# Gate rows by a strided DMA, and nineteen steps of dot products in the second down product

## The chip, the cores and the metric

The kernel runs on one core of a Trainium2 chip. The metric is the device time of one execution in microseconds (us); the median of a few runs is compared. A profile of one execution gives the engines' busy times, their waits and the clock granted to TensorE. The engines are called TensorE (PE in the profile; PEld is its weight load), VectorE (DVE), ScalarE (ACT), GpSimd (POOL) and SyncE (SP, which here only issues DMAs).

## What is computed

One layer of a diffusion backbone: 512 latent tokens and 256 context tokens of width 1024, with shift, scale and gate vectors made from a conditioning vector (`c` for the latent tokens, `c_ctx` for the context). Cut to what matters here:

```python
mod_x = (jax.nn.silu(c) @ w_ada + b_ada).reshape(bsz, N_MOD, 1, d)      # N_MOD = 9 sections of 1024
mod_c = (jax.nn.silu(c_ctx) @ w_ada + b_ada).reshape(N_MOD, 1, d)

def ffn_sublayer(h, m, i, w_up, w_down):
    shift, scale, gate = sub_mod(m, i)                                  # sections 3i, 3i+1, 3i+2
    y = swiglu(modulate(h, shift, scale), w_up, w_down)                 # 1024 -> 2 x 2816 -> 1024
    return post_ln(DEEPNORM_ALPHA * h + 0.5 * gate * y, ln_g[i], ln_b[i])

x = ffn_sublayer(x, mod_x, 0, ffn1_w_in, ffn1_w_out)
ctx = ffn_sublayer(ctx, mod_c, 0, ffn1_w_in, ffn1_w_out)
...                       # neighbourhood attention and gated DeltaNet on sections 3 and 4
x = post_ln(DEEPNORM_ALPHA * x + gate_x * branch_merge(...), ln_g[1], ln_b[1])     # section 5
x = ffn_sublayer(x, mod_x, 2, ffn2_w_in, ffn2_w_out)                    # sections 6, 7, 8
```

The context's output isn't wanted, so the context needs sections 0 to 4 only.

## The kernel before

Matmuls take split operands: a float32 value is written as a high and a low part (`split`, lines 137 and 139: ScalarE casts, VectorE subtracts), and each product is three matmuls. The first half-step's hidden width of 2816 is 22 tiles of 128. The first 8 tiles (`N1`) are computed unit by unit, for the latent tokens and then for the context (`ffn_unit`, lines 192 to 194). Their part of the down projection follows (`down`, line 211): the *first down product*, first for the latent tokens ("x": eight weights, two of them held and used tile by tile at the end), then for the context ("c"). The result goes to DRAM as `accd`. The other 14 tiles (`N2`) are computed by `Seven.run`, a product of seven block products in place of eight (lines 527 to 529); each unit's hidden tile goes to DRAM as `hd`. Then the *second down product* (lines 672 to 674) reads these back as `hx` and `hc`, splits them, and adds the other 14 weights' share: 24 matmuls of 512 columns for a weight, the last six weights (`KL1`) held and used tile by tile. The context's share follows, then the input projection and the mixers.

The conditioning's sections 0 and 1 are made at the start (`modulate_k`). Sections 2 to 8 come from a generator, `ada_gen` (line 291). Each of its 56 steps loads 128 columns of `w_ada` (transposed, 512 KB) into a raw tile, and VectorE multiplies it with a broadcast conditioning row and sums (`dot_cols`, line 281): one dot product for sections 5 to 8, two (latent, context) for sections 2 to 4. The sums stand as columns, 128 partitions by 8, in `colx` and `colc`; at a section's end the bias is added (line 303). `ada_step(n)` runs n steps where it stands in the program. The steps are laid out so: two in the latent units, six in the context units, six in the first down product (`t_sums`, called after each of its first six weights), and 42 in the sevenfold units (`ADA2`).

Gates (sections 2, 5 and 8, and section 2 for the context) are needed as rows along the free dimension. `rows_out` does this for all sections that are ready, at two places: after the context units, and after the sevenfold units. `to_row` transposes 8 columns on TensorE (line 242), scales by 0.5 on ScalarE (line 244) and writes 8 rows of 512 bytes to DRAM (line 245); later a broadcast DMA loads the row for all partitions (lines 564, 248).

Each engine runs its instructions in order, and so does each DMA queue issue its transfers. That order is laid down when the kernel is built: the program's instructions are scheduled against a simulated timeline, so an instruction can be placed ahead of one that stands earlier in the program, if its operands and buffers are ready first by that simulation. SP's queue carries the weights (line 174), the generator's raw tiles (line 297), the hidden tiles (line 656) and the gate rows; POOL's queue carries `hd` and `accd`. Weights come through a `Stream` with two raw tiles and, here, three pairs of split tiles.

The generator's raw tiles during the sevenfold units:

```python
    def raw2():
        raws2[0] += 1
        return tl(tp, [P, D], "wr") if raws2[0] % 2 else tl(sgp, [P, D], "wr")
```

Memory comes in pools that open and close like a stack from either side; a tile in a newly opened pool waits for the last use of what lay there.

Of the kernel before, what the change touches and what calls it, by code (L numbers as in the profile page):

```python
# [12 lines left out]
AF = mybir.ActivationFunctionType  # L13
# [5 lines left out]
P = 128  # L19
D = 1024  # L20
KT = D // P
# [37 lines left out]
def body(ctx, tc, I, out, dbg=None):  # L59
    nc = tc.nc  # L60
    V, S, G, T = nc.vector, nc.scalar, nc.gpsimd, nc.tensor
# [15 lines left out]
    def tl(p, shape, tag, bufs=1, dt=F32):  # L77
        uid[0] += 1
        return p.tile(list(shape), dt, name=f"{tag}_{uid[0]}", tag=tag, bufs=bufs)
# [156 lines left out]
                        after(t, j, banks[t])  # L236
        return banks, tail

    def to_row(sp, pp, cols, row):

        ps = tl(pp, [8, P], "ps", 8)
        T.transpose(ps[:], cols, ident)
        t = tl(sp, [P, D], "adap")[0:8, 0:P]
        S.activation(t, ps[:], AF.Copy, scale=0.5)
        nc.sync.dma_start(row, t)

    def bcast_row(dst, row):
        nc.sync.dma_start(dst[:], row.rearrange("k p -> (k p)")[None].broadcast_to([P, D]))
# [42 lines left out]
    def ada_gen(tps, raw_of, crow):  # L291
        for sec in range(2, 9):
            which = [(0, colx)] + ([(1, colc)] if sec < 5 else [])
            sl = slice(sec * 8, sec * 8 + 8)
            for k in range(KT):
                raw = raw_of[0]()
                nc.sync.dma_start(raw[:], I["w_adaT"][sec * KT + k])
                for w, col in which:
                    dot_cols(tps[0], raw, crow[:, w], col, sec * 8 + k)
                if k < KT - 1:  # L300
                    yield
            for w, col in which:
                V.scalar_tensor_tensor(col[:, sl], col[:, sl], float(sec % 3 == 1), bcol[:, sl], op0=ALU.add, op1=ALU.add)
                if (w, sec) in gates:
                    rows_due.append((w, sec))
            yield

    def secs(col, s):
        return col[:, s * 8:s * 8 + 8]
# [72 lines left out]


    F0, KC, KL1, KL2 = 3, 2, 6, 6
    ADA2 = (2, 2, 2, 2, 3, 3, 3, 4, 4, 4, 4, 4, 5, 0)
    PSB = [2]
    pp0, close_pp0 = pool("pp0", space=PSUM)
    nc.scalar.dma_start(crow[0:1], I["c_row"])
# [51 lines left out]
        xn["c"].append(tl(st0, [P, D], f"x{t}")[:])  # L440
        ln_norm(tp, xn["c"][t], raw, act=True)
    gates = {k: tl(dp, [8, P], "gate")[:] for k in ((0, 2), (1, 2), (0, 5), (0, 8))}
    ada_tp, ada_raw, rows_due = [tp], [raw1], []
    ada = ada_gen(ada_tp, ada_raw, crow)

    def ada_step(n=1):
        for _ in range(n):
            next(ada, None)

    def rows_out(pp):  # L450
        while rows_due:
            w, sec = rows_due.pop(0)
            to_row(ada_tp[0], pp, secs((colx, colc)[w], sec), gates[(w, sec)])

    for f in range(F0, N1):
        hx.append(h_x())
        ffn_unit(tp, pp, ws.get(), ws.get(), uxh, uxl, NX, *hx[-1])
        for k in range(KC * (f - F0), min(KC * (f - F0 + 1), KT)):
            modulate_k(pp, "c", k)
        if f < F0 + 2:  # L460
            ada_step()
    trow = {}

    def sums(k):
# [11 lines left out]
    for f in range(N1):  # L476
        hc.append(h_c())
        ffn_unit(tp, pp, ws.get(), ws.get(), uch, ucl, NCT, *hc[-1])
        ada_step(f < 6)
    rows_out(pp)  # L480
    accd = tl(dp, [6, P, D], "accd")

    def t_sums(j):
        if j < 4:
            sums(j)
        ada_step()

    class Seven:

# [67 lines left out]
                r.prep_b()  # L557

    sraw = [tl(tp, [P, 3, 512], "s")[:].rearrange("p a n -> p (a n)")]
    for kind, n, hs in (("x", 4, hx), ("c", 2, hc)):  # L560
        g = [tl(tp, [P, 512], "fs", 2) for _ in range(2)]
        row = gates[(kind == "c", 2)].rearrange("k p -> (k p)")[None]
        for d in range(2):
            nc.sync.dma_start(g[d][:], row[:, d * 512:(d + 1) * 512].broadcast_to([P, 512]))
        banks, tail = down(pp, ws, hs, n, 2 if kind == "x" else 0, tail if kind == "c" else (), between=t_sums if kind == "x" else None)
        if kind == "c":
            fs = [Seven(N1), Seven(N1 + 1)]
            fs[0].prep_a()
            fs[0].prep_s()
        for t in range(n):  # L570
            xr = tl(hxp, [P, 2, NX], "hx", N1, F32R)[:].rearrange("p a n -> p (a n)").bitcast(F32)
            nc.sync.dma_start(xr, tok_src(kind, t))
            tmp = tl(tp, [P, D], "adap")
            for d in range(2):
                sl = slice(d * 512, (d + 1) * 512)
                V.tensor_tensor(tmp[:, sl], banks[t][d][:], g[d][:], ALU.mult)
                V.scalar_tensor_tensor(xr[:, sl], xr[:, sl], ALPHA, tmp[:, sl], op0=ALU.mult, op1=ALU.add)
            nc.gpsimd.dma_start(accd[t + 4 * (kind == "c")], xr)
# [21 lines left out]
    for f in range(N2):  # L600
# [1 line left out]
        if f + 2 < N2:  # L602
            fs.append(Seven(N1 + f + 2))
        ada_step(ADA2[f])
    for _ in ada:
        pass
    rows_out(pp)
    close_sg()
    close_tp()
    close_up()  # L610
    close_cr()


    accp, close_accp = pool("acc1")
# [53 lines left out]
    def h_next(j):  # L668
        h_split(j + 7)
        h_split_c(2 * j + 2)  # L670

    h_split(4)
    bx, tail = down(pp, ws, hx, 4, KL1, between=h_next, n=N2)
    h_split_c(N2)
    close_hxp()
    ux, close_ux = pool("u2x", "right")
    uc, close_uc = pool("u2c", "right")
# [37 lines left out]
    close_lp()  # L715
    close_hcp()
    close_accp()
    close_wx()


# [1137 lines left out]
```

## Time and profile before

| | |
|---|---|
| median of 3 runs | 1529.88 us (1527.28 to 1530.88) |
| the profiled execution | 1527.83 us, its span 1526.0 us |
| TensorE | 1435.3 us busy, 94% of the span; mean granted clock 0.981 |
| VectorE, ScalarE, GpSimd | 76%, 42%, 14% |
| DMA | 248 MB, 163 GB/s over the span |

A matmul's end is modelled, so TensorE's busy time is read together with the number of matmuls in a window. The share of a busy engine is a mean over stages; the stage at hand is read from windows, waits and timelines. The first half-step runs to about 590 us.

### The profile page before, as it was taken

The page shows a single profiled execution, that of the slowest core. Times are in us where ns is not written, and L with a number is a line of the kernel's source. Part 1 is how long each engine was busy: PE and PEld are TensorE (multiplying, and loading weights), DVE is VectorE, ACT ScalarE, POOL GpSimd, SP SyncE. Part 2 cuts the span into 40 slices and gives each one's busy share as a digit, 9 for nine tenths or more (in the row PEclk, how much of TensorE's full clock was granted, in tenths as well). Part 3 has the DMA queues.
Part 4 walks back from the last instruction along what each step waited for, and adds up shares of the span by engine and source line. Part 5 has one row for each costly group of instructions (what it writes and reads, how often), then busy time and mean ns, then how long its engine had stood idle before and what let it go on. Part 6 is the DMA issues. An engine that isn't in the chain of part 4 may idle for free.

```text
span 1526.0 us, 23870 instructions
## 1 busy us (share of the span) xinstructions
PE 1435.3 (94%) x9118; PEld 1259.0 (83%) x9118; DVE 1155.8 (76%) x1992; ACT 648.1 (42%) x1067; POOL 213.7 (14%) x251
## 2 busy tenths in 40 slices
PE   6998999999957999999996899989999999999997
PEld 4788889999955888898885687867778999998886
DVE  8799869999983487678768886557669699886426
ACT  5444423434332254655633344266516454344310
POOL 0000000000000021233301001233232022220001
PEclk9999999999988999999998999999999999999999
DMA  9675774546677334322377534274354133333422
GB/s 370 205 269 193 256 273 171 174 167 232 213 253 258 129 138 139 112 84 97 109 223 191 173 98 129 73 259 140 100 179 139 56 127 114 106 111 139 138 83 83
DMA packets 114756, 248.03 MB, mean 163 GB/s; under 512 B 35073, under 2 KB 50513, under 8 KB 114641
## 3 DMA queue, kind: packets, MB, share of 16 engines
q1 hardware_dynamic: 109632, 227.30, 44.4%
q0 software_dynamic: 3424, 13.90, 2.4%
q10 hardware_dynamic: 1586, 5.32, 0.9%
q8 instruction: 71, 1.16, 0.3%
q14 instruction: 43, 0.35, 0.1%
HBM read 214.98 MB, written 31.50 MB: 162 GB/s over the span
## 4 chain that ended last, share of the span: by engine, by line
PE 59%; DVE 18%; DMA 9%; issue 9%; ACT 2%; POOL 2%; SPq 1%; DVEq 0%; POOLq 0%; ACTq 0%
PE ps L211 13%; PE pm L192 5%; PE pm L194 5%; PE pm L193 5%; DVE wl L139 4%; DMA wr<-in_w_adaT_dram 3%; PE pc L1015 3%; PE ps L194 3%; PE ps L193 3%; PE ps L192 2%; PE ps L1647 2%; DVE adap L281 2%; PE ps L1645 2%; PE ps L1646 2%; PE ps L527 2%
## 5 line engine op out<-in xcount | busy, mean ns | idle before, releaser
L139 DVE TENSOR_TENSOR wl<-wr,wh 128x1024 fp32r<-128x1024 f32 (+1 forms) x185 | 226.0, 1225 | 127.8 <-ACT wh L137 127.4
L137 ACT CAST wh<-wr 128x1024 fp32r<-128x1024 f32 (+1 forms) x185 | 186.6, 1013 | 275.5 <-PE ps L211 59.8
L192 PE MATMUL pm<-uxh,wh 128*128 128x512 f32 x320 | 132.1, 413 | 0.3 <-ACT spill L764 0.3
L194 PE MATMUL pm<-uxh,wl 128*128 128x512 f32 x320 | 127.0, 397 | 0.7 <-DVE wl L139 0.7
L193 PE MATMUL pm<-uxl,wh 128*128 128x512 f32 x320 | 126.9, 397 | 0.0
L281 DVE SCALAR_TENSOR_TENSOR adap<-wr,crow 128x1024 f32<-128x1024 f32 x89 | 109.1, 1225 | 12.7 <-DMA wr<-in_w_adaT_dram 8.8
L114 POOL TENSOR_TENSOR rs<-ve,mhalf 128x1 f32<-128x1 f32 (+2 forms) x46 | 52.2, 1137 | 327.3 <-DVE ve L110 320.1
L211 PE MATMUL ps<-wh,hx 128*128 128x512 f32 x352 | 96.4, 394 | 0.0
L211 PEld LDWEIGHTS ps<-wh,hx 128*128 128x128 f32 x352 | 66.7, 190 | 13.9
L194 PE MATMUL ps<-uh,wl 128*128 128x256 f32 (+1 forms) x208 | 67.8, 326 | 6.2 <-DVE wl L139 6.2
L194 PEld LDWEIGHTS pm<-uxh,wl 128*128 128x128 f32 x320 | 60.9, 190 | 14.7 <-DVE wl L139 1.7
L192 PEld LDWEIGHTS pm<-uxh,wh 128*128 128x128 f32 x320 | 61.0, 191 | 12.0 <-ACT spill L764 0.9
L193 PEld LDWEIGHTS pm<-uxl,wh 128*128 128x128 f32 x320 | 61.1, 191 | 10.3
L192 PE MATMUL ps<-uh,wh 128*128 128x256 f32 (+1 forms) x208 | 67.6, 325 | 0.0
L193 PE MATMUL ps<-ul,wh 128*128 128x256 f32 (+1 forms) x208 | 67.1, 322 | 0.0
L193 PE MATMUL ps<-uxl,wh 128*128 128x256 f32 (+1 forms) x192 | 61.0, 320 | 0.9 <-DVE uxl L139 0.9
L194 PE MATMUL ps<-uxh,wl 128*128 128x256 f32 (+1 forms) x192 | 60.6, 319 | 0.0
L192 PE MATMUL ps<-uxh,wh 128*128 128x256 f32 (+1 forms) x192 | 60.4, 321 | 0.0
L137 ACT CAST wh<-ra 128x1024 fp32r<-128x1024 f32 x30 | 31.5, 1052 | 63.3 <-PE ps L211 24.1
L527 PE MATMUL ps<-uh,wh 128*128 128x384 f32 x168 | 56.7, 338 | 1.4 <-ACT ur L541 1.4
L527 PE MATMUL ps<-ur,wh 128*128 128x384 f32 x168 | 56.5, 336 | 0.0
L528 PE MATMUL ps<-ur,wh 128*128 128x384 f32 x168 | 56.4, 336 | 0.0
(482 smaller groups left out, 4215.3 us busy)
## 6 DMA issues: line engine op xcount, KB each, us to landing
wr<-in_w_adaT_dram SPq DMA_DIRECT2D x70, 512.0 KB, 4.1
wr<-in_up_dram SPq DMA_DIRECT2D x56, 512.0 KB, 4.2
wr<-in_dn_dram SPq DMA_DIRECT2D x52, 512.0 KB, 3.2
wr<-in_win_dram SPq DMA_DIRECT2D x52, 512.0 KB, 3.6
ra<-in_up_dram SPq DMA_DIRECT2D x24, 512.0 KB, 4.0
ra<-in_w_adaT_dram SPq DMA_DIRECT2D x18, 512.0 KB, 4.9
rb<-in_up_dram SPq DMA_DIRECT2D x18, 512.0 KB, 3.7
wr<-in_w_o_dram SPq DMA_DIRECT2D x8, 512.0 KB, 4.5
```

What stands on the lines that cost most here:

```text
L114: G.tensor_tensor(rs[:], ve[:], mhalf[:, 0:n], ALU.pow)
L137: S.copy(hi, src)
L139: V.tensor_tensor(lo, src, hi.bitcast(F32), ALU.subtract)
L192: T.matmul(ps, a, uh[:, k, :], start=(k == 0), stop=False)
L193: T.matmul(ps, a, ul[:, k, :], start=False, stop=False)
L194: marks["mm"] = T.matmul(ps, b, uh[:, k, :], start=False, stop=(k == nk - 1)).ins
L211: T.matmul(banks[t][d][:, c0:c1], a[:, sl], b[:, d * 512 + c0:d * 512 + c1], start=first and j == 0, stop=last and j == 2)
L281: V.scalar_tensor_tensor(pr[:], raw[:], 1.0, crow, op0=ALU.mult, op1=ALU.mult, accum_out=col[:, c:c + 1])
L527: T.matmul(ps[:], a, mh, start=k == 0, stop=False)
L528: T.matmul(ps[:], a, ml, start=False, stop=False)
L1015: last[0] = T.matmul(*a, **k).ins
L1645: T.matmul(ps[:], a, uh[:, k], start=k == 0, stop=False)
```

## The change

`to_row` no longer uses TensorE: ScalarE copies and scales the 128 x 8 columns into a small tile, and a DMA with a rearranged destination writes them to the 8 rows, element by element. It is called as soon as a section is complete; `rows_due` and `rows_out` are gone. The steps of the generator are laid out anew: one after the latent units, four in the context units (every other one), six in the first down product, 26 in the sevenfold units (two in each but the last), and 19 in the second down product (3, 3, 3, 2, 2, 2, 2, 2 after its first eight weights), from two raw tiles and a product tile of a pool of their own (`ada1`). The gate row for the latent tokens' first eviction is loaded after the fourth weight of the first down product instead of ahead of it. The pool of the conditioning rows (`cr`) is closed later.

```diff
-    def to_row(sp, pp, cols, row):
-
-        ps = tl(pp, [8, P], "ps", 8)
-        T.transpose(ps[:], cols, ident)
-        t = tl(sp, [P, D], "adap")[0:8, 0:P]
-        S.activation(t, ps[:], AF.Copy, scale=0.5)
-        nc.sync.dma_start(row, t)
+    def to_row(sp, cols, row):
+
+        t = tl(sp, [P, KT], "row")
+        S.activation(t[:], cols, AF.Copy, scale=0.5)
+        nc.sync.dma_start(row.rearrange("k p -> p k"), t[:])
...
                 if (w, sec) in gates:
-                    rows_due.append((w, sec))
+                    to_row(tps[0], col[:, sl], gates[(w, sec)])
...
-    ADA2 = (2, 2, 2, 2, 3, 3, 3, 4, 4, 4, 4, 4, 5, 0)
+    ADA2 = (2,) * 13 + (0,)
+    ADA3 = (3, 3, 3, 2, 2, 2, 2, 2)
...
-        if f < F0 + 2:
-            ada_step()
+    ada_step()
...
-        ada_step(f < 6)
-    rows_out(pp)
+        ada_step(1 - f % 2)
...
         ada_step()
+        if j == 3:
+            load_g(0)
...
-    for kind, n, hs in (("x", 4, hx), ("c", 2, hc)):
-        g = [tl(tp, [P, 512], "fs", 2) for _ in range(2)]
-        row = gates[(kind == "c", 2)].rearrange("k p -> (k p)")[None]
+    g = []
+
+    def load_g(w):
+        g[:] = [tl(tp, [P, 512], "fs", 2) for _ in range(2)]
+        row = gates[(w, 2)].rearrange("k p -> (k p)")[None]
         for d in range(2):
             nc.sync.dma_start(g[d][:], row[:, d * 512:(d + 1) * 512].broadcast_to([P, 512]))
+
+    for kind, n, hs in (("x", 4, hx), ("c", 2, hc)):
+        if kind == "c":
+            load_g(1)
...
-    for _ in ada:
-        pass
-    rows_out(pp)
     close_sg()
     close_tp()
     close_up()
-    close_cr()
...
     def h_next(j):
         h_split(j + 7)
         h_split_c(2 * j + 2)
-
+        ada_step(ADA3[j])
+
+    ad, close_ad = pool("ada1")
+    ada_tp[0], ada_raw[0] = ad, lambda: tl(ad, [P, D], "wr", 2)
     h_split(4)
     bx, tail = down(pp, ws, hx, 4, KL1, between=h_next, n=N2)
     h_split_c(N2)
+    for _ in ada:
+        pass
+    close_ad()
...
     close_accp()
+    close_cr()
     close_wx()
```

More of the change, by code (lines that the diff above doesn't have):

```diff
@@ L442, in body @@
     gates = {k: tl(dp, [8, P], "gate")[:] for k in ((0, 2), (1, 2), (0, 5), (0, 8))}
-    ada_tp, ada_raw, rows_due = [tp], [raw1], []
+    ada_tp, ada_raw = [tp], [raw1]
     ada = ada_gen(ada_tp, ada_raw, crow)
@@ L448, in ada_step @@
             next(ada, None)
[L450 to L453, printed above, removed]
     for f in range(F0, N1):
```

## The prediction, made before the changed kernel was run

> **What bounds the kernel now.** I read the page's busy shares first, then the waits of TensorE stage by stage, then the windows around the one long wait, then the timelines of the engines inside it.
>
> ```profile
> span 1526.0 us, 23870 instructions
> ...
> PE 1435.3 (94%) x9118; PEld 1259.0 (83%) x9118; DVE 1155.8 (76%) x1992; ACT 648.1 (42%) x1067; POOL 213.7 (14%) x251
> ...
> core 0: us, PE busy (x) PEld busy (x) DVE busy (x) ACT busy (x) POOL busy (x), PEclk, DMA share, GB/s
> 243.00:442.00 199.00, 197.55 (x1134) 196.61 (x1133) 194.13 (x313) 75.80 (x100) 7.05 (x13) 1.00 0.56 192
> 442.00:470.00 28.00, 1.68 (x6) 1.20 (x5) 20.89 (x41) 8.57 (x19) 2.50 (x5) 0.55 0.82 280
> 470.00:546.00 76.00, 76.00 (x332) 62.77 (x331) 34.41 (x47) 16.92 (x19) 5.74 (x7) 0.99 0.45 163
> 480.00:520.00 40.00, 40.00 (x178) 33.13 (x177) 14.31 (x14) 12.49 (x14) 0.00 (x0) 1.00 0.49 170
> ```
>
> TensorE is the bound nearly everywhere, but from 442 to 470 us it does 1.68 us of work in 28. The stage before (the 14 sevenfold units, 243 to 442) keeps it full, although VectorE is 97% busy there; the stage after (the second down product) leaves VectorE 42 us of room. The hole between them is one wait:
>
> ```profile
> engine line waited for: us in total, times, longest us
> PE ps L242 <- DVE colx L303: 26.3, 1, 26.3
> ...
> 442.01 0.27 PE L242 MATMUL ps<-ident,colx 128*8 128x128 f32 x1
> ...
> 468.60 0.37 PE L242 MATMUL ps<-ident,colx 128*8 128x128 f32 x1 [26.32 <-DVE colx L303]
> 468.63 1.20 PE L211 MATMUL ps<-wh,hx 128*128 128x512 f32 x2
> ...
> L281 DVE SCALAR_TENSOR_TENSOR adap<-wr,crow x8: 1216/1225/1226, 441.2 to 466.8; 128x1024 f32<-128x1024 f32 x8
> ...
> 468.30 0.16 DVE L303 SCALAR_TENSOR_TENSOR colx<-colx,bcol 128x8 f32<-128x8 f32 x1
> ```
>
> The transposes of two gate rows (line 242) stand in TensorE's queue between the last unit and the down product's first matmul (line 211, 0.03 us after the second). The second waits for section 8's last dot product: eight dots are still to do at 441.2 us, and they come at (466.8 - 441.2) / 7 = 3.66 us apiece, paced by a load and two raw tiles in turn. Nothing else holds the down product: see the next step.
>
> **The change, step by step.** Steps are counted as the generator yields them: 56, of which 24 have two dots.
>
> *1. The transposes leave TensorE (gain 26.3).* Gate rows now go by an ACT copy and a strided DMA; no matmul waits for a column sum any more. What is late next?
>
> ```profile
> 439.07 1.22 DVE L139 TENSOR_TENSOR wl<-wr,wh 128x1024 fp32r<-128x1024 f32 x1
> ...
> 445.30 1.22 DVE L139 TENSOR_TENSOR wl<-wr,wh 128x1024 fp32r<-128x1024 f32 x1
> ...
> 452.50 0.55 DVE L553 TENSOR_TENSOR c<-c,ps 128x384 f32<-128x384 f32 x1
> ```
>
> The first down weight is split at 440.3, the second at 446.5; one weight is 24 matmuls of 40 / 178 = 0.225 us, 5.4 us, so the second is due at 447.4: in time. The last unit's last product left PSUM only at 453.05, 11 us after TensorE had made it (442.0), because VectorE was behind; the down product's first weight reaches that bank, the last of its eight, at about 446.5. Left as it is, that costs 6.5 us. But units 7 to 12 (counted from 0) now carry two dots where they carried four (one five): 13 dots fewer in the stage, 13 x 1.22 = 16 us less for VectorE, more than the 11 us. I take 0, bound 6.5.
>
> *2. The slow restart (gain 2).*
>
> ```profile
> 460.00:465.00 5.00, 0.00 (x0) 0.00 (x0) 3.49 (x9) 2.19 (x6) 0.00 (x0) 0.50 1.04 397
> ...
> 470.00:472.00 2.00, 2.00 (x6) 1.56 (x5) 0.00 (x0) 0.02 (x1) 0.70 (x2) 0.50 0.92 346
> 472.00:476.00 4.00, 4.00 (x18) 3.26 (x18) 0.00 (x0) 0.00 (x0) 0.00 (x0) 0.99 0.86 317
> ...
> L211 PE MATMUL ps<-wh,hx x352: 387/389/776, 170.1 to 546.3; 128*128 128x512 f32 x176
> ```
>
> The granted clock falls to 0.50 in the wait and comes back at 472. The down product's 336 matmuls take 468.6 to 546.5, 77.9 us, where 336 x 0.225 is 75.5. Without the wait those 2.4 us go; I take 2.
>
> *3. Three steps leave the first half-step's units (gain 2).*
>
> ```profile
> PE ps L194 <- DVE wl L139: 6.2, 6, 1.7
> ```
>
> These six waits, all in the first half-step's units, are for weight splits that stand behind dots on VectorE. Eight steps before the first down product become five: of two in the latent units' loop one is left, behind it, and of six in the context units four. That is 3 x 2 x 1.22 = 7.3 us less for VectorE. The gain lies between 0 (if the dots that leave ran where the matmuls had weights enough) and 6.2; I take 2. ACT's copies of rows are as many as before.
>
> *4. Section 2 ends later, its rows go strided (0, bound 13).* It now ends three steps into the first down product.
>
> ```profile
> 171.37 0.35 SPq L245 DMA_DIRECT2D gate<-adap  x1
> ...
> 173.36 0.34 SPq L564 DMA_DIRECT2D fs<-gate  x1
> ...
> 186.76 1.23 DVE L281 SCALAR_TENSOR_TENSOR adap<-wr,crow 128x1024 f32<-128x1024 f32 x1
> ...
> 205.52 1.29 DVE L576 TENSOR_TENSOR adap<-ps,fs 128x512 f32<-128x512 f32 x2 [0.19 <-PE ps L211]
> ...
> L211 PEld LDWEIGHTS ps<-wh,hc x176: 186/188/192, 213.5 to 589.4; 128*128 128x128 f32 x176
> ...
> L1105 SPq DMA_DIRECT2D Ltr<-bd x6: 319/447/556, 776.5 to 872.6; - x6
> ...
> DMA to landing us min/median/max: 3.0/3.3/3.7
> ...
> L564 SPq DMA_DIRECT2D fs<-gate x4: 320/334/386, 173.4 to 215.0; - x4
> ...
> DMA to landing us min/median/max: 3.4/4.0/4.5
> ...
> L248 SPq DMA_DIRECT2D gx<-gate x2: 327/327/327, 1125.7 to 1397.8; - x2
> ...
> nw<-in_norm_w_dram SPq DMA_DIRECT2D x1, 0.5 KB, 4.1
> ```
>
> In the profile the stage's third step has its last dot at 186.8 to 188; the same place holds section 2's last dot afterwards. Then ACT 0.3, the strided write, the load of the row (4.0, and another queued behind): the eviction wants it at 205.5. The write has 128 x 8 pieces of 4 bytes. The row with as many pieces is the transposed read of line 1105, 1024 pieces of 128 bytes, 3.3 us; the row with pieces as small is norm_w, 128 of 4 bytes, 4.1 us, eight times which is 33. With 3.3 the rows are there at about 197, 8 us early; I take that end, the row nearest in number of pieces, and 0. With 33 they come at 226, the eviction of the first tile (1.3 us) frees banks at 227 and the context product, due at 213.5, waits 13 us. SP waits for the write before it can load the row, and weight loads stand behind that; they run two weights (10.8 us) ahead, so 3.3 us of it cost nothing. The rows of sections 5 and 8 are first read at 1125 and 1397 us.
>
> The Trainium skill, page "DMA: Bandwidth & Descriptors", section "Rules for kernel authors", speaks against this step: a strided last dimension is cut into one descriptor per element, and a plain rearranged DMA is put at a 19-fold cost beside a hardware transpose. Taking 19 times the old row write (2.0 us from its issue to its reader's, 171.4 to 173.4) gives an estimate of 38 us, an 18 us stall instead of 0 and 1523.5 us in all; line 1105's 3.3 us for 1024 pieces speaks against it, and no run yet shows 4-byte writes.
>
> *5. Nineteen steps move into the second down product (cost 6, from 0 to 26).* They are 19 dots of 1.22 = 23 us on VectorE, which has 42 us free, 19 issues of 0.33 us on SP, and 19 loads of 0.52 MB. The 14 context splits, which ran in the hole, add 5 us there.
>
> ```profile
> wr<-in_w_adaT_dram SPq DMA_DIRECT2D x70, 512.0 KB, 4.1
> ...
> L139 DVE TENSOR_TENSOR hc<-hc 128x256 fp32r<-128x256 f32 x14 | 5.3, 422 | 2.5 <-ACT hc L137 2.5
> ...
> 442.46 3.28 SPq L297 DMA_DIRECT2D wr<-in_w_adaT_dram  x2
> ...
> 446.31 2.11 SPq L656 DMA_DIRECT2D hc<-hd  x4
> ...
> 462.55 0.33 SPq L297 DMA_DIRECT2D wr<-in_w_adaT_dram  x1
> ```
>
> The transfers decide. From 442 to 546 us the profile moves 28 x 280 + 76 x 163 GB/s = 20.2 MB, with six of these loads in it (442.5 to 462.6). Afterwards it is 13 more, 27 MB, in the 76 us that the product takes: 356 GB/s, where the fullest rows above show 317 to 397. At 340 it is 80 us, 4 more than the matmuls. By pace: 19 x 3.66 = 70 us, where the program puts the steps beside the first eight weights, 43 us. Were the queues to keep program order, weights would lag by 26; with two weights in hand, by 16. But the order is not that of the program: above, loads of the context's tiles, later in the program, are issued among the dots' loads, and half of the product (six weights held for all tiles) comes after. So I take 6, near the bandwidth end.
>
> *6. The rest (0).*
>
> ```profile
> POOL ax L617 <- DVE colx L303: 11.8, 1, 11.8
> ...
> PE ps L527 <- ACT ur L541: 1.4, 2, 1.1
> ```
>
> ACT and POOL have room (17 and 6 of 76 us). POOL's loads of the accumulators waited 11.8 us for the same sum, off the path; they start earlier. In the sevenfold units TensorE waited 1.4 us, so less VectorE work gives nothing there. Every later stage begins earlier and is otherwise as before.
>
> **Sum.** Span 1526.0, own time 1527.8 us. 1527.8 - 26.3 - 2 - 2 + 6 = 1503.5. The median of the runs, 1529.9, lies 2.0 above the profiled execution's time: 1505.5.
>
> **Rivals.**
> - *Half of the gain lost in the down product.* The planned order ties weight splits to dots that wait for a crowded DMA: a lag of 16 instead of 6, 1515.5. For it: the two raw tiles' pace and 356 GB/s. Against: two weights ahead, and VectorE's room.
> - *Slower than before.* SP keeps program order: a load for a dot waits for its raw tile, and the product's weights wait behind. The lag is 26, and the six held weights start loading only after the last step: 6 x 0.52 MB at 340 GB/s, 9.2, and two splits 2.4. 1499.5 + 38 = 1537.5. It decides from a stall of 33 us on.
> - *The row is late.* The strided write takes 33 us: 1505.5 + 13 = 1518.5. It costs TensorE time from a landing of 20 us on (188.5 + 20 + 4 reaches 212.5, one eviction before 213.5). By the skill's rule above this case would be 1523.5.
> - *The wait only changes its name.* Something else, the evictions of step 1 and first loads bunched at 442 us, holds TensorE for most of those 26 us: about 1528. Against it: both first weights were split before they were due.
>
> **How the numbers follow.** Forecast 0.63; half lost 0.17; slower 0.07; late row 0.05; new name for the wait 0.04; better still (no stall, step 3's full 6 us, 1495) 0.04. The forecast's own range is 1496 to 1513. For 8 in 10 the range runs from 1494 to 1524, through the lost half and the late row. A measurement here tells about 0.2%, 3 us, from no change: faster 0.88, same 0.04, slower 0.08.
>
> **What would show it.** Right: no wait of TensorE above 5 us between the last unit and the down product, granted clock 1.0 there, the down product's start near 440 us, and some 75 to 85 us for it; DMA share above 0.8 in that stretch. Step 3: a sum below 6 us on the weight splits of line 139 before the first down product. Step 4: the strided writes landing within 5 us, and no wait of the first evictions for the row. Wrong: TensorE waiting for splits of line 139 by more than 15 us during the down product, or for the first evictions.

## The result, and the profile after

The changed kernel is slower, where it was forecast to be faster: 1544.34 us median (1541.91 to 1547.91, 4 runs) against 1530.38 us before (1527.28 to 1531.58, 4 runs), a ratio of 1.0096 with a 95% interval of 1.0071 to 1.0121. The profiled execution took 1547.91 us, 3.6 above its median.

The page of the changed kernel opens so (span, then busy time and share of the engines):

```profile
span 1546.1 us, 23871 instructions
...
PE 1447.1 (94%) x9114; PEld 1266.2 (82%) x9114; DVE 1156.1 (75%) x1992; ACT 648.7 (42%) x1067; POOL 211.0 (14%) x251
```

Busy shares are those of before; they say nothing on where 20 us went. For that the span is cut at four matmuls. The groups of TensorE by line, of the kernel before (count, duration in ns, first and last start):

```profile
L211 PE MATMUL ps<-wh,hc x176: 388/389/499, 213.7 to 589.6; 128*128 128x512 f32 x176
...
L192 PE MATMUL pm<-uxh,wh x320: 389/389/795, 618.8 to 1010.1; 128*128 128x512 f32 x160
```

and of the changed kernel:

```profile
L211 PE MATMUL ps<-wh,hx x352: 387/389/628, 169.0 to 539.4; 128*128 128x512 f32 x176
...
L211 PE MATMUL ps<-wh,hc x176: 388/389/628, 225.9 to 591.7; 128*128 128x512 f32 x176
...
L192 PE MATMUL pm<-uxh,wh x320: 387/389/795, 633.5 to 1029.8; 128*128 128x512 f32 x160
```

The first start with `hx` is the start of the first down product, the first with `hc` the end of its latent part, the last with `hx` the end of the second down product's latent part; `pm` is the second set of columns of the input projection, the stage behind the normalizations of the first half-step. Every run below is cut at the same rows (us, one profiled execution each):

| kernel | to the first down product | its latent part (A) | its context part, the sevenfold units and the second down product's latent part (B) | from there to `pm` (C) | rest (D) | span |
|---|---|---|---|---|---|---|
| before | 170.1 | 43.6 | 332.6 | 72.5 | 907.2 | 1526.0 |
| after | 169.0 | 56.9 | 313.5 | 94.1 | 912.6 | 1546.1 |
| difference | -1.1 | +13.3 | -19.1 | +21.6 | +5.4 | +20.1 |

The gain that was forecast is there, in B. It is outweighed by losses in A and C, where the forecast had 0. The waits of TensorE in the changed kernel (total us, times, longest):

```profile
PE ps L211 <- DVE wl L139: 18.1, 5, 8.7
...
PE ps L192 <- ACT uxh L137: 6.4, 1, 6.4
PE ps L521 <- ACT c L530: 5.0, 1, 5.0
...
PE ps L194 <- DVE wl L139: 4.2, 5, 1.4
```

The wait on the transposes is gone. New are the down products' waits for weight splits (first row), the input projection's wait for its input, and one of 5.0 us in a sevenfold unit. Their origin, in A, is read from the queues. The timeline of SP, ScalarE, VectorE and TensorE (start, duration, engine, line; in brackets the idle time before it and what ended that):

```profile
183.00 0.39 SPq L243 DMA_DIRECT2D gate<-row  x1
...
195.60 0.33 SPq L560 DMA_DIRECT2D fs<-gate  x1
196.03 0.38 SPq L243 DMA_DIRECT2D gate<-row  x1
...
195.69 0.21 ACT L242 ACTIVATE row<-colc 128x8 f32<-128x8 f32 x1 [11.87 <-DMA gate<-row]
...
210.45 1.04 ACT L137 CAST wh<-ra 128x1024 fp32r<-128x1024 f32 x1 [12.39 <-DMA ra<-in_dn_dram]
...
208.94 1.22 DVE L279 SCALAR_TENSOR_TENSOR adap<-ra,crow 128x1024 f32<-128x1024 f32 x1 [10.84 <-DMA ra<-in_w_adaT_dram]
...
212.63 1.22 PE L211 MATMUL ps<-wl,hx 128*128 128x512 f32 x2 [8.74 <-DVE wl L139]
```

The strided write of the first row is issued at 183.0 and the load that needs it at 195.60: 12.6 us. SP's queue stood for that time, and ScalarE too, since the second row's copy (195.69) reuses the one `row` tile; weight casts stand behind it. Then the second row goes out at 196.03, and now VectorE sits idle for 10.8 us until a raw tile comes, ScalarE for 12.4 until a weight comes; both loads were issued within 1.6 us of that write. All four writes, by their line:

```profile
L243 SPq DMA_DIRECT2D gate<-row x4: 378/378/385, 183.0 to 539.4; - x4
...
DMA to landing us min/median/max: 9.2/10.8/12.6
```

The third and the fourth do the same further on:

```profile
413.92 0.38 SPq L243 DMA_DIRECT2D gate<-row  x1
...
418.64 0.54 POOL L549 DMA_DIRECT2D hd<-c  x1 [12.99 <-DVE c L548]
...
430.98 0.48 ACT L530 COPY c<-ps 128x384 f32<-128x384 f32 x1 [9.01 <-DMA hd<-c]
...
539.43 0.38 SPq L243 DMA_DIRECT2D gate<-row  x1
539.90 1.33 SPq L251 DMA_DIRECT2D lng<-in_ln_g_dram  x1
...
550.83 1.28 DVE L257 SCALAR_TENSOR_TENSOR ax<-ax,bmv,lng 128x1024 f32<-128x1024 f32 x1 [7.17 <-DMA lng<-in_ln_g_dram]
```

A hidden tile's write on POOL's queue, issued 4.7 us behind the third row (413.9), holds ScalarE's next copy, and with it the unit, until 430.98: a transfer of another queue is late too. Behind the fourth, the layer norm's first load holds VectorE for 7.2 us.

So the first theory: the strided write is slow, and while it lasts it holds the other transfers. The rival: what is slow is SP's order, in which loads stand behind the write. Still another part of C had nothing to do with the write, as the runs showed.

### The profile page after: what moved, and what is told of

Its sections match the earlier page's. It is cut to its first block, busy times and chain, and to the rows that moved or that the text cites. A ratio compares the mean times of both kernels' runs of the same rounds, so it can differ in the third digit from the quotient of the medians.

```text
span 1546.1 us, 23871 instructions
## 1 busy us (share of the span) xinstructions
PE 1447.1 (94%) x9114; PEld 1266.2 (82%) x9114; DVE 1156.1 (75%) x1992; ACT 648.7 (42%) x1067; POOL 211.0 (14%) x251
## 3 DMA queue, kind: packets, MB, share of 16 engines
q1 hardware_dynamic: 113728, 227.30, 45.4%
## 4 chain that ended last, share of the span: by engine, by line
PE 48%; DVE 17%; DMA 16%; issue 14%; ACT 3%; POOL 2%; SPq 1%; DVEq 0%; POOLq 0%; ACTq 0%
PE ps L211 9%; PE pm L192 4%; PE pm L194 4%; PE pm L193 4%; DMA wr<-in_dn_dram 4%; DVE wl L139 3%; PE ps L1649 3%; PE ps L1648 3%; PE ps L1650 3%; PE pc L1018 2%; PE ps L192 2%; PE ps L194 2%; PE ps L193 2%; DVE adap L279 2%; DMA wr<-in_w_adaT_dram 2%
## 5 line engine op out<-in xcount | busy, mean ns | idle before, releaser
L279 DVE SCALAR_TENSOR_TENSOR adap<-wr,crow 128x1024 f32<-128x1024 f32 x86 | 104.7, 1218 | 18.2 <-DMA wr<-in_w_adaT_dram 17.5
L211 PE MATMUL ps<-wl,hx 128*128 128x512 f32 x176 | 56.1, 398 | 9.3 <-DVE wl L139 9.3
L522 PE MATMUL ps<-ul,wh 128*128 128x384 f32 x168 | 57.1, 340 | 0.0
L523 PE MATMUL ps<-uh,wl 128*128 128x384 f32 x168 | 57.1, 341 | 0.0
## 6 DMA issues: line engine op xcount, KB each, us to landing
wr<-in_w_adaT_dram SPq DMA_DIRECT2D x69, 512.0 KB, 4.5
wr<-in_up_dram SPq DMA_DIRECT2D x57, 512.0 KB, 3.3
wr<-in_dn_dram SPq DMA_DIRECT2D x53, 512.0 KB, 3.8
wr<-in_win_dram SPq DMA_DIRECT2D x52, 512.0 KB, 3.5
ra<-in_up_dram SPq DMA_DIRECT2D x23, 512.0 KB, 4.0
ra<-in_w_adaT_dram SPq DMA_DIRECT2D x19, 512.0 KB, 4.6
rb<-in_up_dram SPq DMA_DIRECT2D x18, 512.0 KB, 3.6
wr<-in_w_o_dram SPq DMA_DIRECT2D x8, 512.0 KB, 4.3
```

Source lines behind the costliest of these rows:

```text
L211: T.matmul(banks[t][d][:, c0:c1], a[:, sl], b[:, d * 512 + c0:d * 512 + c1], start=first and j == 0, stop=last and j == 2)
L279: V.scalar_tensor_tensor(pr[:], raw[:], 1.0, crow, op0=ALU.mult, op1=ALU.mult, accum_out=col[:, c:c + 1])
L522: T.matmul(ps[:], a, ml, start=False, stop=False)
L523: T.matmul(ps[:], b, mh, start=False, stop=k == 3)
```

## The experiments

The kernel before was run again with each group: 1526.6 us with e1 to e4, 1531.0 with e5 to e8, 1530.3 with e9 to e12 and 1530.5 with e13 to e15 (medians). Ratios are to those. Since the same kernel differs by 4.4 us between groups, a difference of two medians of different groups is sure to about that much only; where it matters, the difference against each group's own kernel before stands beside it.

With pieces of 8 or 32 bytes a row's values land in another order. So e1, e5, e8 to e11, e13 and e14 serve to time the stages, but don't compute the layer; e2, e3, e4, e6, e7, e12 and e15 do.

**The size of the pieces.** First, the same bytes in longer pieces, and the same pieces from another queue.

```diff
 # e1_long_pieces, after's to_row: 128 pieces of 32 bytes
-        nc.sync.dma_start(row.rearrange("k p -> p k"), t[:])
+        nc.sync.dma_start(row.rearrange("k p -> (k p)").rearrange("(p k) -> p k", k=KT), t[:])
 # e2_act_queue, after's to_row
+        nc.scalar.dma_start(row.rearrange("k p -> p k"), t[:])
```

> The changed kernel, with one edit: each gate row is written in 128 pieces of 32 bytes, not 1024 of 4 (the row's values land in another order; all else is the same). Theory A (the 1024-piece write holds up every transfer behind it): the writes land in 2 to 4 us instead of 9 to 12.6, TensorE's 8.7 us wait in the first down product and the 5.0 us wait in the sevenfold units go, lng arrives 7 us earlier, and the time is 1510 to 1525. Theory B (the nineteen steps in the second down product are what costs): 1535 to 1545, hardly below the changed kernel's 1544.

> The changed kernel, with the strided writes issued from ScalarE's queue instead of SP's. Theory A1 (the write occupies the DMA engines that all queues share; a POOL write issued 5 us after one took 12.3 us): loads on SP are as late as before, 1538 to 1548. Theory A2 (only what stands behind it in SP's own queue is late): 1512 to 1527. Theory B: 1540 to 1548.

| kernel | A | B | C | D | median us | ratio to before, 95% interval |
|---|---|---|---|---|---|---|
| e1: 32-byte pieces | 43.9 | 308.4 | 88.0 | 908.5 | 1520.54 | 0.995 (0.9929 to 0.9971) |
| e2: ACT's queue | 57.4 | 309.7 | 95.8 | 906.2 | 1541.66 | 1.0094 (1.0058 to 1.013) |

Longer pieces take 23.8 us off the changed kernel (20.0 against each group's kernel before) and bring it 0.5% below the kernel before; another queue changes next to nothing. The writes of e1 and of e2:

```profile
DMA to landing us min/median/max: 1.4/2.6/5.4
...
DMA to landing us min/median/max: 10.4/12.3/13.1
```

The theory of SP's order falls. The Trainium skill, page "DMA: Bandwidth & Descriptors", section "Issuing engines are not separate DMA queues", says that DMAs issued by ScalarE, SyncE or GpSimd end up on the same 16 DMA engines; A of 57.4 us in e2 against 56.9 in the changed kernel agrees. How they are held shows in windows (the last two columns are the DMA share and GB/s), of the changed kernel:

```profile
186.00:194.00 8.00, 8.00 (x37) 6.64 (x36) 3.77 (x7) 0.00 (x0) 0.00 (x0) 1.00 1.09 60
```

and of e1:

```profile
186.00:194.00 8.00, 8.00 (x37) 6.64 (x36) 5.57 (x8) 2.21 (x3) 0.00 (x0) 1.00 0.84 296
```

In both, the DMA engines are shown as busy (shares of 1.09 and 0.84); with the 4-byte write they move a fifth of the bytes. The single packets in the changed kernel's trace tell more. Within 1.2 us, from 185.0 on, 1056 packets of under 512 bytes start, the row's 1024 pieces and a few others, each recorded as about 9 ns long; in the 8.8 us after that only 13 do. What fills the engines then is the 4096-byte packets of other transfers: the median of the 117 that start from 186 to 194 us lasts 1.13 us, where 0.16 is the median of the whole run. Behind the third write it looks otherwise, but comes to the same: 1040 small packets start from 414.3 to 415.6 us, only 49 packets of any kind in the 8.4 us after that, and the share from 413.9 to 424 is 0.19, at 20 GB/s. So the pieces leave within one to two microseconds, and the stall of the others comes behind them. What holds them is not shown.

Is it the number of pieces, or their size? e1 changed both. Three runs part them: e8 writes the row in 512 pieces of 8 bytes; e9 and e10 add to e1 a write that nobody reads, of 512 pieces of 4 bytes and of 1024 pieces of 8.

```diff
 # e8_half_pieces, after's to_row
+        nc.sync.dma_start(row.rearrange("k p -> (k p)").rearrange("(a p k) -> p a k", a=4, k=2), t[:].rearrange("p (a k) -> p a k", k=2))
 # e9_scratch_512x4, behind e1's row write
+        scr = tl(dp, [4, P], "scr")
+        nc.sync.dma_start(scr[:].rearrange("k p -> p k"), t[:, 0:4])
 # e10_scratch_1024x8, behind e1's row write; t2 holds each value twice
+        scr = tl(dp, [KT, P, 2], "scr")
+        nc.sync.dma_start(scr[:].rearrange("k p a -> p k a"), t2[:])
```

> The changed kernel with 512 pieces of 8 bytes for a gate row instead of 1024 of 4 (values in another order). If the write costs by the piece: it lands in 5 to 8 us where the 1024 pieces took 9 to 12.6, and the time is about half way between 1544 and 1520.5: 1528 to 1537. If any piece under 32 bytes costs the same in sum: as the changed kernel, 1540 to 1546.

> The changed kernel with 32-byte pieces (1520.5), and behind each gate row an added write of half of the columns to a place that nobody reads, in 512 pieces of 4 bytes. The rows of 512 pieces of 8 bytes landed in 3.2 to 3.6 us and delayed nothing, the 1024 of 4 bytes in 9 to 12.6. If the size of a piece decides: the added writes take 5 to 7 us and cost half of what the 1024 did, 1528 to 1534. If the number decides, and 512 are few enough: 3 to 4 us, 1518 to 1524.

> As before, but the added write has 1024 pieces of 8 bytes (each value twice). If the number of pieces decides: it lands in 9 to 12 us, and holds the loads behind it as the rows of 4-byte pieces did, 1538 to 1546. If pieces of 4 bytes are what is slow: 5 to 7 us, and 1518 to 1526.

The landings of the writes in question, in e8, e9 and e10:

```profile
DMA to landing us min/median/max: 3.2/4.7/7.0
...
DMA to landing us min/median/max: 10.0/10.6/12.4
...
DMA to landing us min/median/max: 4.9/5.0/7.0
```

| kernel | pieces | A | B | C | D | median us | ratio, 95% interval |
|---|---|---|---|---|---|---|---|
| e8 | 512 of 8 bytes | 45.4 | 308.1 | 87.2 | 907.9 | 1519.72 | 0.9922 (0.9898 to 0.9945) |
| e9 | 512 of 4 bytes, added | 56.7 | 315.4 | 95.7 | 912.5 | 1550.46 | 1.0125 (1.0108 to 1.0143) |
| e10 | 1024 of 8 bytes, added | 45.9 | 309.3 | 93.4 | 910.3 | 1528.7 | 0.999 (0.9973 to 1.0007) |

It is the size. 512 pieces of 4 bytes bring the whole loss back, and 1024 pieces of 8 bytes, with the same number as the changed kernel's write and twice its bytes, a fifth to a third of it (8.2 us over e1, 4.4 against each group's kernel before; e10 also has one more copy on ScalarE for each row). Neither e8 nor e9 came out as either of its theories said: e8 lay below both, e9 above both; e8's landings go up to 7.0 us, where e9's expectation says 3.6. e10 landed as the theory of small pieces said, and took 2.7 us more than its range. That 512 pieces of 4 bytes last as long as 1024 was in neither theory, and why is open; so is what makes 4 bytes so much dearer than 8.

Where the loss falls is told by the changed kernel with only its first two rows, those of section 2, in 32-byte pieces.

```diff
+        if sec == 2:
+            row = row.rearrange("k p -> (k p)").rearrange("(p k) -> p k", k=KT)
+        else:
+            row = row.rearrange("k p -> p k")
```

> The changed kernel, with only the two writes of section 2 in 128 pieces of 32 bytes; those of sections 5 and 8 stay at 1024 pieces of 4 bytes. Section 2's rows hold their values in another order, so its output is not the reference's. Theory (each write costs at its own place): the first latent down product comes back from 56.9 to about 43.7 us and the time to 1544.3 - 13 = 1531; the remaining 10.5 us over the run with all rows in 32 bytes (1520.5) is the two later writes, about 5 in the sevenfold units and 5 to 7 behind the second down product. Rival 1 (the time saved in front is taken back behind, since a later wait ends at the same moment): 1541 or more. Rival 2 (the two later writes cost nothing, and all of the difference lies in front): 1520 to 1523.

It took 1537.61 us (1.0052, 1.0036 to 1.0069): A 43.9, B 316.0, C 96.9, D 908.4. In the profiled executions the first two writes cost 13.0 (A), the third 7.6 (B, against e1) and the fourth 8.9 (C); in the medians the first two are worth 6.7 and the others 17.1 (the changed kernel's profiled execution was 3.6 above its median). Against each group's kernel before, the medians give 6.9 and 13.1. Neither rival holds, and the time lies above the theory's 1531: A came back as foretold, but B and C are 2.5 and 2.8 us longer than in the changed kernel, so part of what is saved in front is taken back behind. The two later writes, which the prediction passed over as not needed for a long time, are the larger part.

**The same change elsewhere.** The strided write in the kernel before, with the steps as they were (sections written as soon as they are complete, no `rows_out`), in 4-byte and in 32-byte pieces; and rows made on VectorE by transposing 32 x 32 blocks, written by four DMAs of 8 pieces of 128 bytes.

```diff
 # e4_old_layout (before); e5_old_long the same with e1's write
-    def to_row(sp, pp, cols, row):
+    def to_row(sp, cols, row):
...
+        t = tl(sp, [P, KT], "row")
+        S.activation(t[:], cols, AF.Copy, scale=0.5)
+        nc.sync.dma_start(row.rearrange("k p -> p k"), t[:])
 # e3_dve_rows (after)
+        t, u = rowp, tl(sp, [P, 32], "row")
+        S.activation(t[:, 0:KT], cols, AF.Copy, scale=0.5)
+        V.transpose(u[:], t[:])
+        for b in range(4):
+            nc.sync.dma_start(row[:, 32 * b:32 * b + 32], u[32 * b:32 * b + KT, :])
```

> The changed kernel, with the columns transposed by VectorE in 32 x 32 blocks, and each row written by four DMAs of 8 pieces of 128 bytes. It computes what the reference does. Theory A: as with the 32-byte pieces, 1510 to 1525, and faster than the kernel before by 0.3 to 1.3%. Theory B: 1535 to 1545.

> The kernel before, with only the new way of writing gate rows (ScalarE copy and strided DMA as soon as a section ends); the steps stay where they were, none in the second down product. Theory A: the 26 us wait on the transpose goes, but two strided writes before the first down product and one in the sevenfold units cost some 10 to 15: 1510 to 1522. Theory B: the full gain, 1498 to 1506. If neither the strided writes nor the steps cost anything by themselves but only together: 1498 to 1506 too, with writes landing in 9 to 12 us.

> The kernel before with gate rows written as soon as a section ends, in 128 pieces of 32 bytes (the row's values land in another order); the steps stay where they were, none in the second down product. Read it beside the same with 1024 pieces of 4 bytes (1547) and beside the changed kernel with 32-byte pieces (1520.5). Theory A (the pieces of 4 bytes are the whole loss): 1520 to 1528 less than 1547 by 20 to 28, and the input projection's first matmul at 565 to 575 us. Theory C (beside the pieces, the nineteen steps hold up the layer norm behind the second down product: 576.6 with them): without them the first matmul of the input projection at 560 to 568. From there on this build's order of instructions differs from before's, as in the run with 4-byte pieces, where that part took some 10 us longer.

| kernel | start | A | B | C | D | median us | ratio, 95% interval |
|---|---|---|---|---|---|---|---|
| e3 | 170.3 | 44.8 | 310.8 | 86.8 | 920.7 | 1535.2 | 1.0044 (1.0025 to 1.0063) |
| e4 | 188.1 | 43.6 | 324.3 | 74.9 | 917.5 | 1546.96 | 1.0136 (1.0105 to 1.0167) |
| e5 | 170.8 | 43.5 | 306.4 | 75.2 | 918.7 | 1515.3 | 0.9889 (0.9871 to 0.9908) |

e4 and e5 differ in the pieces alone: 31.7 us (36.1 against each group's kernel before), of which 17.3 in the profiled executions now lie ahead of the first down product, where section 2 ends in the old layout. e4 is far above every time that was expected of it (1522 at most), e5 below its 1520 to 1528. e5 also has C at 75: without the moved steps C is nearly as before (72.5). e3 has A, B and C about as e1 (44.8, 310.8 and 86.8); it missed its 1510 to 1525 by D, 13.5 us over before, in stages that no edit touched (below).

**The wait without the strided write, and without moved steps.** The kernel before, with only the second `rows_out` moved behind the second down product's context part: its transposes no longer stand ahead of that product.

```diff
 # e6_late_rows (before)
         pass
-    rows_out(pp)
     close_sg()
...
     down(pp, ws, hc, 2, 0, tail[:-NT], between, after, post=tail[-NT:], n=N2)
+    rows_out(lambda: tl(lp, [P, 512], "h1", 2), pp)
 # e7_late_rows_new: e6, and 16 steps in the second down product, with the pool ada1
+    ADA2 = (2,) * 13 + (0,)
+    ADA3 = (2,) * 8
 # e12_late_rows_nine: e7 with 9 steps there
+    ADA2 = (2,) * 6 + (3,) * 7 + (0,)
+    ADA3 = (2, 1, 1, 1, 1, 1, 1, 1)
 # e15_late_rows_nineteen: e7 with 19
+    ADA2 = (2,) * 10 + (1, 1, 1, 0)
+    ADA3 = (3, 3, 3, 2, 2, 2, 2, 2)
 # e14_long_sixteen: e1 with 16
+    ADA2 = (3,) * 3 + (2,) * 10 + (0,)
+    ADA3 = (2,) * 8
 # e11_ln_early: e1 with the layer norm's rows loaded ahead of the product
+    lng, lnb = load_ln(lp, 0)
```

> The kernel before, with one edit: the second call of rows_out (gate rows of sections 5 and 8, TensorE transposes as before) stands behind the second down product's context part instead of ahead of the product. No step is moved, no strided write. If the 26.3 us wait is all that these transposes cost: the input projection's first matmul at 560 to 566 us instead of 589.9, and 1500 to 1512 in all (the part behind it may lose up to 10 us, since its order of instructions differs). If the wait only changes its name: 580 to 590 us, and 1520 to 1535.

> As the kernel with the late rows, and sixteen steps of dot products moved into the second down product (two after each of its first eight weights; 26 stay in the sevenfold units). Theory C (steps there delay the evictions and the layer norm): the input projection's first matmul 6 to 14 us later than with the late rows alone. Theory D (the move helps, since VectorE is freed in the sevenfold units): no later, or some us earlier. Total by A and C 1505 to 1520.

> As the kernel with the late rows, TensorE transposes and sixteen steps in the second down product (1505.3), but with nine steps there, and three instead of two in each of the sevenfold units 6 to 12, where VectorE has room. Theory C (each step there delays the layer norm): the input projection's first matmul at 560 to 564 us instead of 566.5, and 1500 to 1504, if the later stages keep their order of instructions; up to 10 more if not.

> The kernel with the old row writes, of which the second pair comes behind the second down product, and with 19 steps moved (3, 3, 3, 2, 2, 2, 2, 2) where the fastest version has 16; the three come out of the last sevenfold units. Theory (number of steps): 53 to 55 us from the end of the latent part to the input projection where 16 steps had 44.0, and 1513 to 1516. Rival (the row written behind the last dot): 44 to 45 us, and 1504 to 1507.

> The changed kernel with all rows in 128 pieces of 32 bytes (values in another order), and with 16 of the dot products' steps beside the second down product instead of 19 (three more beside the first sevenfold units). Theory (VectorE's layer norms stand behind the last dots, and three steps fewer let two of the tiles through in time): from the end of the second down product's latent part to the input projection 44 to 47 us where the run with 19 steps had 54.6, and a time of 1510 to 1513. Rival (the nine us come from the row written behind the last dot and the loads queued after it, whatever the number of steps): 53 to 55 us there, and 1519 to 1522.

> The changed kernel with 32-byte pieces, and the two layer norm rows (lng, lnb) in tiles of their own in a pool that opens ahead of the second down product, so that their load doesn't wait for the generator's last dot product (there 519.4 us, load at 522.5, first use 527.8; first matmul of the input projection 576.6). If that load is what holds up the layer norm: first use at 514 to 518, the input projection at 566 to 571, and 1510 to 1516. If it is the evictions, which stand among the dots on VectorE: the first use still at 524 to 527, and no faster than 1518.

| kernel | steps moved | A | B | C | D | median us | ratio, 95% interval |
|---|---|---|---|---|---|---|---|
| e6 | 0 | 43.6 | 305.2 | 73.0 | 915.2 | 1509.53 | 0.9864 (0.9845 to 0.9882) |
| e12 | 9 | 43.6 | 308.1 | 78.8 | 917.8 | 1521.06 | 0.993 (0.9908 to 0.9952) |
| e7 | 16 | 43.6 | 308.0 | 73.0 | 907.2 | 1505.3 | 0.9827 (0.9813 to 0.9842) |
| e15 | 19 | 43.6 | 308.1 | 89.2 | 907.2 | 1521.94 | 0.9945 (0.993 to 0.9961) |
| e14 | 16, strided in 32 bytes | 43.6 | 305.8 | 75.1 | 917.3 | 1514.5 | 0.9904 (0.9885 to 0.9922) |
| e1 | 19, strided in 32 bytes | 43.9 | 308.4 | 88.0 | 908.5 | 1520.54 | 0.995 (0.9929 to 0.9971) |
| e11 | 19, strided in 32 bytes | 43.6 | 309.4 | 86.6 | 909.4 | 1519.66 | 0.9929 (0.9914 to 0.9944) |

e7 is the fastest version: 1505.3 us (1504.47 to 1505.73), 1.7% below the kernel before and 2.5% below the changed one (1505.3 / 1544.34 = 0.975).

e15 against e7 is the cleanest pair: A, B and D agree within 0.1 us, but C, with three steps more, is 16.2 us longer (88.0 against 75.1 in e1 and e14, by the other way of writing rows). The three steps are 3 x 1.22 us of dots. From the end of the latent part to the input projection's first matmul it is 54.3 us in e15, as its theory said, 44.0 in e7, and 45.4 in e14, as its theory said. Line 257 or 258 is the first instruction of a layer norm's scaling, one for each of the four latent tiles, on VectorE. Between the end of the second down product's latent part and the input projection (busy time, mean ns, idle time before it), in e14:

```profile
L257 DVE SCALAR_TENSOR_TENSOR ax<-ax,bmv,lng 128x1024 f32<-128x1024 f32 x3 | 3.8, 1274 | 0.0
```

and in e15, with the wait of TensorE in the same stretch:

```profile
L258 DVE SCALAR_TENSOR_TENSOR ax<-ax,bmv,lng 128x1024 f32<-128x1024 f32 x4 | 5.1, 1275 | 0.0
...
PE ps L192 <- ACT uxh L137: 9.3, 1, 9.3
```

With 19 steps all four layer norms are still to do when the latent part ends; with 16, three. In the kernel before it is two, but in e6 and e5, where no step was moved, it is three as well: what 19 steps push behind the product is one layer norm more. In e15 the last dot runs until 520.0 us, in e7 until 512.0:

```profile
518.85 1.23 DVE L280 SCALAR_TENSOR_TENSOR adap<-wr,crow 128x1024 f32<-128x1024 f32 x1
...
524.40 1.28 DVE L258 SCALAR_TENSOR_TENSOR ax<-ax,bmv,lng 128x1024 f32<-128x1024 f32 x1
...
552.73 1.27 DVE L258 SCALAR_TENSOR_TENSOR ax<-ax,bmv,lng 128x1024 f32<-128x1024 f32 x1
...
572.41 2.90 ACT L151 ACTIVATE u<-ps,colx 128x128 f32<-128x128 f32 x8 [0.42 <-DVE uxl L139]
```

and in e7:

```profile
510.85 1.22 DVE L280 SCALAR_TENSOR_TENSOR adap<-wr,crow 128x1024 f32<-128x1024 f32 x1
...
517.59 1.27 DVE L258 SCALAR_TENSOR_TENSOR ax<-ax,bmv,lng 128x1024 f32<-128x1024 f32 x1
...
546.09 1.28 DVE L258 SCALAR_TENSOR_TENSOR ax<-ax,bmv,lng 128x1024 f32<-128x1024 f32 x1
...
562.45 2.90 ACT L151 ACTIVATE u<-ps,colx 128x128 f32<-128x128 f32 x8 [3.14 <-DVE x1c L625]
```

The first and the last layer norm of the latent tiles start 6.8 and 6.6 us later in e15, and the last tile's modulation (line 151), which in e15 also waits for VectorE's split of an earlier tile, 10.0; its cast is the input for which TensorE waited. That split stands on VectorE behind work for the context's tiles, which by now has become ready too. From the end of the latent part to the input projection VectorE is busy for 52.2 of 54.3 us in e15, for 38.6 of 44.0 in e7. In e15 the two late rows are scaled on ScalarE just ahead of that modulation, in e1 they are not, and e1 has the same wait:

```profile
573.16 2.90 ACT L151 ACTIVATE u<-ps,colx 128x128 f32<-128x128 f32 x8 [2.98 <-DVE uxl L139]
```

Of C's 16.2 us 10.3 lie ahead of the input projection's first matmul. The other 5.9 are behind it: a second wait of TensorE, 3.3 us, and a slow start after the first one, with a granted clock of 0.57 from 575.9 to 581 us.

So between 16 and 19 the number of steps is shown as the cause; the rival, the row written behind the last dot, falls by e15, which has no such write, and by e14, which has one and no such loss. e11 shows that the late load of the layer norm's rows is not it either (C 86.6). The times of e15 and e14, 1521.9 and 1514.5, lie above what that theory gave (1513 to 1516 and 1510 to 1513). And the loss doesn't grow evenly with the steps. C is 73.0 with no step moved (e6) and with 16 (e7; there the input projection came 4.3 us later than in e6, where theory C had 6 to 14). With nine (e12, expected at 1500 to 1504 us) it is 78.8. In e12 TensorE waited 3.6 us for a weight split behind a cast, in another order of instructions. Fewer is not simply better.

D has two levels: 906 to 913 us in before, after, e1, e2, e7 to e11, e13 and e15, and 915 to 921 in e3, e4, e5, e6, e12 and e14. In the traces of the first group SP issues its last 330 of 577 transfers in the order of the kernel before; in those of the second only the last 55 or 112 agree, though no edit lies there: the planned order of late stages tips over with small edits far ahead of them. All 17 profiled kernels fall in line, but no run changed that order alone, so it is a correlation. It would account for e14 ending 9.2 us above e7 (1514.5 - 1505.3), with D 10.1 longer, and only 6.0 below e1, though its C is 12.9 shorter.

## Why the prediction was wrong, step by step

*Step 1, the transposes leave TensorE (gain 26.3), and step 2, the slow restart (2).* Right. e6 has this alone: B falls by 27.4 us, of 28.3 forecast. The bound of 6.5 for evictions behind VectorE was not drawn on.

*Step 3 (gain 2).* The first down product started 1.1 us earlier in after, and in its variants between 0.6 earlier and 1.3 later (e8 and e9); the sum on the weight splits fell from 6.2 to 4.2 in after, and to 5.0 in e1. About half of the gain is there at most.

*Step 4, the rows go strided (0, bound 13).* This is the step that turned the sign. Between two rows it took the one with as many pieces (1024 of 128 bytes, 3.3 us) rather than the one with as small ones (4.1 us for 128 of 4 bytes). Both rows are loads; the write goes to DRAM. Measured: 9.2 to 12.6 us a row. So the row nearest in size pointed the right way, though its eightfold, 33 us, was about three times too high, and e9 shows that the time doesn't go with the number of pieces (512 as long as 1024). By the prediction's own formula 12.6 us would still have been free: 188.5 + 12.6 + 4 = 205.1, ahead of the 205.5 at which the eviction wants the row. The formula was wrong, too: it asked when the row is read and what stands behind the write on SP's queue, and never what shares the DMA engines and ScalarE with it. So the rows of sections 5 and 8, "first read at 1125 and 1397 us", were given no price, and cost more than the first two. All four cost 20.0 to 23.8 us in the medians (after against e1). The rule of the Trainium skill, page "DMA: Bandwidth & Descriptors", section "Rules for kernel authors", that a strided last dimension becomes one descriptor per element, spoke rightly against the step: 1040 packets under 512 bytes start within 1.3 us behind the third write, near one for each of 1024 elements. The factor of 19 that stands there is against a hardware transpose, which no run here has. The prediction took it against the old row write and estimated 38 us; against that write it was 4.6 to 6.3 here (9.2 to 12.6 against 2.0). The rival of the late row had the right culprit, but not the path, and so a price of 13.

*Step 5, nineteen steps in the second down product (6, 0 to 26).* Inside the product it was right: B is 3.2 us longer in e1 than in e6, which moved none, and the product's latent part ran 80.2 us against 76.9, as the bandwidth sum said. What failed is "which has 42 us free" of VectorE: the room was counted up to the product's end, but the evictions and layer norms at its end were delayed by the dots. One layer norm more than without them was pushed behind the product, and the others came later, into a stage where VectorE then has next to no room (in e15 52.2 of 54.3 us busy). That is C: 15.5 us in e1 over before. The prediction put it into step 6, "every later stage begins earlier and is otherwise as before", at 0.

*Sum.* Of the 38.8 us between forecast and median, 23.8 are step 4 (20.0 against each group's kernel before); the other 15.0 are 1520.54 - 1505.5, and in e1's profile C alone is 15.5. Of the signs that the prediction named, the down product's length of 75 to 85 us (78.2) came, while its start near 440 us (461.2; 441.8 in e1) and the landing within 5 us did not. That e7 comes out at 1505.3 is no proof of the sum: it has other row writes and 16 steps. The forecast of a slower kernel (0.08) had its loss in the wrong place, the weights behind SP's loads: TensorE waited only 1.9 to 2.5 us in the second down product in after, e7 and e15.

## What to carry to other kernels

Price a scattered write by the size of its pieces first, and charge it to every transfer and every buffer that is under way while it lasts, not only to its own reader; an added write that no one reads, as in e9, shows the whole price. When work is moved into an engine's free time, count what ran in that time until now and where it goes: e7 and e15 differ by three dots, 3.7 us of VectorE, and by 16.6 us. And try the smallest edit that removes a wait: moving one call (e6) brought nearly all that steps 1 and 2 had promised in B (27.4 of 28.3 us), and 1.4% in all, since D was 8.0 longer.

## What was not expected of the hardware

512 pieces of 4 bytes took 10.0 to 12.4 us to land (e9), as long as 1024 of them (9.2 to 13.1 in after and e2, up to 18.4 in e4), while 512 of 8 bytes took 3.2 to 7.0 (e8) and 1024 of 8 bytes 4.9 to 7.0 (e10). The small pieces themselves start within 1.2 to 1.8 us; for 8 to 10 us behind them transfers of SP's and POOL's queues were held up. Behind the first write the 16 DMA engines showed as busy meanwhile, with 4096-byte packets of 1.13 us (median) instead of 0.16, and moved 60 GB/s instead of 296; behind the third they showed a share of 0.19, at 20 GB/s.
